# Order of the last retention head's rows and of the second feed-forward's first weights in a two-layer transformer kernel

## The chip, the cores and the metric

The kernel runs on one core of one Trainium2 chip. Its time is the device time of one execution in microseconds, taken over several runs; the median is given. All arithmetic is fp32 in effect: each large fp32 operand is split into a rounded high part (`hi`, made by ScalarE, type fp32r) and the remainder (`lo`, made by VectorE), and one product is three matmuls: hi x hi, lo x hi, hi x lo.

The engines are named as in the profile: PE (TensorE matmuls), PEld (its weight loads), DVE (VectorE), ACT (ScalarE), POOL (GpSimd) and SP (SyncE, which issues the transfers). SBUF is the on-chip memory, PSUM the eight banks into which PE writes.

## The reference

Two layers of a diffusion backbone over 512 latent tokens of width 1024 with 256 context tokens. Layer 0 is windowed attention with a feed-forward, for latent and context tokens; layer 1 is a bidirectional retention mixer with a feed-forward, for the latent tokens alone. The change lies at the end of the mixer of layer 1 and the start of its feed-forward:

```python
def gated_out(o, g):                      # per head: 512 columns
    mu = jnp.mean(o, axis=-1, keepdims=True)
    var = jnp.mean(jnp.square(o - mu), axis=-1, keepdims=True)
    y = ((o - mu) * lax.rsqrt(var + EPS)).reshape(...) * gn_gain
    return (jax.nn.silu(g) * y) @ w_o
...
x = x + mx[2] * out_x
h = modulate(rms_norm(x, norm2_g[i]), mx[3], mx[4])
gate, up = jnp.split(h @ w_in, 2, axis=-1)
x = x + mx[5] * ((jax.nn.silu(gate) * up) @ w_out)
```

The mixer has 4 heads, the feed-forward 2816 hidden columns, which are 22 tiles of 128.

## The kernel before

**Who sets the order.** The kernel is written as a straight program, and a planner (the tile scheduler) gives each engine its own queue: among the instructions that could start by its model it prefers those that stand first in the program. It adds the semaphore waits that the data and the buffers need. `after(ins, others)` adds an edge that orders the plan only: `ins` is not planned before `others`. On one engine this fixes the order in the queue; between two engines it puts no wait into the program. Each engine executes its queue strictly in order, so an instruction whose operand is late holds up all behind it.

**Weights.** All weights come as 128x1024 fp32 blocks in one stream (`w_raw`), mostly into two buffers `wraw`. ACT casts a block to its high part (`whi`), DVE subtracts for the low part (`wlo`), and only then is the raw buffer free for the next transfer on SP's queue. `next_w` (L136 to L142) does these three steps; `first_weights` (L1594) does them for the first weights of the feed-forward, `split` (L164 to L166) does the two computing steps for a block that is there.

**The last head (L1500 to L1585).** `ov` are four PSUM banks (X, X, Y, Y) with the retention output of four groups of 128 tokens, normalised in place (L1530). `gate` are the four gate tiles; the first two still need the product `Zg` added (L1562). `gated(n)` is a silu on ACT and a multiplication on DVE (L1536) that reads `ov[n]`, whose bank is then free. `transposes(i)` turns the gated tiles of tokens half i on PE (L1547) into banks `tps`: four banks X, X, Y, Y for e = 0 to 3, each with all 512 tokens. `turned(c)` splits the turned rows of half c, scaled by the norm's gain, into `yt[e]`: ACT the high part (L1552), DVE the low part (L1553). In the last head the half with tokens 256 to 511 is turned first and the other behind the fourth output tile.

**The output tiles (L1574 to L1630).** `out_tile(d, c)` makes 12 matmuls (L148, L149, L150 through `mm3`) for columns tile d and token half c, into banks pj and Z for the first half made (tokens 256 to 511) and X and Y for the other, and DVE adds the result to the residual stream (L1582). The weights of the eight tiles are four blocks, `w`. Among the tiles stand the squares for the second norm (L207 to L210), its scale (`rms`: a matmul with ones L217, then Ln, Exp and Square on ACT at L101 and L196, and two DVE steps L197 and L198) and the norms `second_norm` (L239 and L243 on DVE, L242 on ACT).

**The feed-forward (L1632 on).** `first_two` makes the hidden tiles f = 0 and 1, first for tokens 256 to 511 and then, behind `second_half` (scale and norms of the other tokens), for tokens 0 to 255. The hidden tile f = 2 is made by `plain`, all later ones by `seven`, a scheme of seven quarter products (L908) with sums of tokens (`token_sums`, L1228 to L1241, into `sA`) and of weights (`quarter_sums`, L915 to L918). `output` multiplies a group of hidden tiles with the output weights into the two pj banks and adds them to the residual stream on DVE (L253). In program order `output` of the first group stands between `plain` for f = 2 and `seven` for f = 3.

## Time and profile before

| | |
|---|---|
| median of 3 runs | 1764.6 us (1764.58 to 1765.39) |
| profiled execution | 1763.84 us |
| its span, first to last instruction | 1762.1 us |
| mean granted TensorE clock | 0.995 |
| PE busy | 1716.5 us (97%) |
| DVE busy | 1335.7 us (76%) |
| ACT busy | 844.1 us (48%) |
| POOL busy | 121.0 us (7%) |

Times in the profile are microseconds from the span's start. A timeline row has the start, the duration, engine, line, operation, written tile <- read tiles, shape, count, and in brackets the idle time of the engine before it with the engine, tile and line that ended it. A row with x2 or x3 merges so many instructions. A row of waits has the waiting engine, tile and line, what it waited for, the total, the number and the longest. Matmuls are pipelined: they start every 0.12 us (256 columns) or 0.23 us (512 columns), and a row's duration of 0.28 or 0.39 us overlaps the next.

### The profile page before, as it was taken

Reading aid. Unit: us, or ns where it says so; the run is one execution under the profiler, and the core shown is the slowest. Engines: PE = TensorE matmul, PEld = TensorE weight load, DVE = VectorE, ACT = ScalarE, POOL = GpSimd, SP = SyncE. Lnnn points to the kernel's source line nnn. Section 1 sums busy time; section 2 is a strip of 40 time slices with the busy share of each in tenths; the row PEclk is TensorE's granted clock in tenths of the full one; section 3 lists DMA queues with packets and bytes.
Section 4 is the critical chain, followed back from the end, with each engine's and each line's share of the span. In section 5 each row is a group of like instructions: output and inputs, shape, how many; then the busy total and the mean of one; then the engine's idle time right before and its main releaser. Section 6 shows DMA issues by size and latency. Waiting matters only on the chain. (4 is left out here: it accounts for less than half of the span.)

```text
span 1762.1 us, 28136 instructions
## 1 busy us (share of the span) xinstructions
PE 1716.5 (97%) x11082; PEld 1535.7 (87%) x11082; DVE 1335.7 (76%) x2373; ACT 844.1 (48%) x1504; POOL 121.0 (7%) x267
## 2 busy tenths in 40 slices
PE   6999999999999999999998999999999999999999
PEld 4788787889999999999987888897897889999998
DVE  6687786478778787877899758758768897777774
ACT  5467786364434333343565534524525564445442
POOL 0014344000000000000000000000000000000000
PEclk9999999999999999999999999999999999999999
DMA  9510014143343434343433434434433323233322
GB/s 354 224 49 14 18 59 153 49 132 108 96 132 124 140 121 155 108 144 128 124 110 122 155 104 128 153 109 132 145 107 109 96 85 115 89 108 108 98 83 84
DMA packets 60900, 205.67 MB, mean 117 GB/s; under 512 B 6752, under 2 KB 7136, under 8 KB 60640
## 3 DMA queue, kind: packets, MB, share of 16 engines
q1 hardware_dynamic: 53856, 178.71, 30.8%
q0 software_dynamic: 6912, 25.17, 4.6%
q8 instruction: 87, 1.43, 0.3%
q14 instruction: 45, 0.37, 0.1%
HBM read 201.75 MB, written 2.10 MB: 116 GB/s over the span
## 5 line engine op out<-in xcount | busy, mean ns | idle before, releaser
L165 ACT CAST whi<-wraw 128x1024 fp32r<-128x1024 f32 x173 | 181.4, 1051 | 309.0 <-PE Z L150 71.0
L166 DVE TENSOR_TENSOR wlo<-wraw,whi 128x1024 fp32r<-128x1024 f32 x173 | 211.1, 1222 | 36.1 <-ACT whi L165 35.5
L908 PE MATMUL Y<-aq,whi 128*128 128x384 f32 x640 | 173.9, 336 | 1.2 <-ACT hn L1049 1.2
L253 DVE SCALAR_TENSOR_TENSOR res<-pj,mod,res 128x512 f32<-128x512 f32 (+1 forms) x102 | 74.3, 730 | 77.7 <-PE pj L150 76.8
L141 DVE TENSOR_TENSOR wlo<-wraw,whi 128x1024 fp32r<-128x1024 f32 x77 | 94.1, 1222 | 34.6 <-ACT whi L140 32.9
L908 PEld LDWEIGHTS Y<-aq,whi 128*128 128x128 f32 x640 | 116.6, 188 | 3.0 <-ACT hn L1049 2.3
L140 ACT CAST whi<-wraw 128x1024 fp32r<-128x1024 f32 x77 | 80.9, 1050 | 74.5 <-PE Z L150 22.5
L271 DVE CUSTOM_DVE_ANT_0 y<-adaw,crow,small_sb 128x1024 bf16<-128x1024 f32 x64 | 81.9, 1280 | 34.4 <-DMA adaw<-in_adaT_dram 34.2
L908 PE MATMUL Y<-aq,wlo 128*128 128x384 f32 x320 | 107.1, 335 | 0.0
L1293 PE MATMUL Z<-whi,sA 128*128 128x512 f32 x256 | 80.7, 391 | 0.0
L101 ACT ACTIVATE pr<-pr,stat,qs 128x513 f32<-128x513 f32 (+2 forms) x96 | 74.2, 775 | 12.3 <-DVE stat L691 9.7
L698 POOL TENSOR_SCALAR pr<-pr,stat 128x512 f32<-128x512 f32 (+2 forms) x96 | 65.5, 696 | 76.4 <-DVE stat L695 57.5
L148 PE MATMUL pj<-ax,whi 128*128 128x512 f32 x176 | 68.8, 391 | 1.7 <-DVE res L253 1.7
L150 PE MATMUL pj<-ax,whi 128*128 128x512 f32 x176 | 68.6, 390 | 0.0
L149 PE MATMUL pj<-ax,wlo 128*128 128x512 f32 x176 | 68.5, 389 | 0.0
L268 POOL DMA_DIRECT2D adaw<-in_adaT_dram x48 | 25.6, 533 | 515.4 <-DVE mod L271 420.8
L148 PE MATMUL pj<-act,whi 128*128 128x512 f32 (+1 forms) x156 | 60.0, 385 | 0.4 <-DVE res L1122 0.4
L908 PE MATMUL Y<-sA,whi 128*128 128x256 f32 x304 | 60.3, 282 | 0.0
L908 PEld LDWEIGHTS Y<-aq,wlo 128*128 128x128 f32 x320 | 60.1, 188 | 0.1
L149 PE MATMUL pj<-act,wlo 128*128 128x512 f32 (+1 forms) x156 | 59.9, 384 | 0.0
L150 PE MATMUL pj<-act,whi 128*128 128x512 f32 (+1 forms) x156 | 59.5, 382 | 0.0
L685 DVE CUSTOM_DVE_ANT_0 pr<-S,mask,qs 128x256 f32<-128x256 f32 (+1 forms) x96 | 52.5, 567 | 8.3 <-PE S L684 5.1
(561 smaller groups left out, 5307.7 us busy)
## 6 DMA issues: line engine op xcount, KB each, us to landing
wraw<-in_wst_dram SPq DMA_DIRECT2D x234, 512.0 KB, 3.7
adaw<-in_adaT_dram POOLq DMA_DIRECT2D x48, 512.0 KB, 3.9
wx<-in_wst_dram SPq DMA_DIRECT2D x28, 512.0 KB, 3.9
adan<-in_adaQ_dram SPq DMA_DIRECT2D x16, 512.0 KB, 8.2
adan<-in_adaN_dram SPq DMA_DIRECT2D x16, 512.0 KB, 8.0
res<-in_xT_dram SPq DMA_DIRECT2D x16, 256.0 KB, 4.8
q<-in_adaN_dram SPq DMA_DIRECT2D x16, 256.0 KB, 3.3
aq<-in_adaN_dram SPq DMA_DIRECT2D x12, 256.0 KB, 6.2
```

The costliest lines, as they stand in the source:

```text
L101: ins = nc.scalar.activation(*args, **kw)
L140: nc.scalar.copy(hi, raw)
L141: nc.vector.tensor_tensor(lo, raw, hi, op=sub)
L148: after(nc.tensor.matmul(o, whi, xhi, start=first, stop=False), behind)
L149: nc.tensor.matmul(o, wlo, xhi, start=False, stop=False)
L150: return nc.tensor.matmul(o, whi, xlo, start=False, stop=last)
L165: nc.scalar.copy(hi, t)
L166: return nc.vector.tensor_tensor(lo, t, hi, op=sub)
L253: return nc.vector.scalar_tensor_tensor(res[d], o, mods[l, s][:, part, d:d + 1], res[d], mult, add)
L271: after(nc.vector.tensor_tensor_reduce(junk, w, cr[:, s * 1024:(s + 1) * 1024], 1.0, sm_t[:, C_ADAB + l * 48 + j:C_ADAB + l * 48 + j + 1], ...
L908: ins = nc.tensor.matmul(o, p, r, start=first and k + i == 0, stop=k == 3 and i == 2, skip_group_check=not first)
L1293: ins = nc.tensor.matmul(o, p, r, start=first and k + i == 0, stop=k == 3 and i == 2, skip_group_check=not first)
```

## The change

- `transposes` in the last head: tokens half 1 is turned into the two Y banks and half 0 into the two X banks, two rows e to a bank, 256 columns each, instead of four banks with 512 columns each for both.
- `turned` returns the last high and low part. In the last head the addition to gate[1] is ordered behind the last low part of half 1, the third output weight's cast behind its last high part, the fourth's behind the gating of gate[1].
- The low parts of the second pair of feed-forward weights are ordered behind the norms 6 and 7 of tokens half 1.
- The casts of the weights for f = 2 are ordered behind the Square in the scale of half 0, the token sums behind norm 7.
- In `seven` for f = 3 the low part of `u` is ordered behind the first residual addition of the first output, that of `g` behind the second.

No instruction is added or removed.

```diff
--- before.py
+++ after.py
@@ -133,11 +133,11 @@
         wsel[0] += 1
         return T(pool, 1024, "whi", bufs, F32R), T(pool, 1024, "wlo", bufs, F32R)
 
-    def next_w(pool, own=2, raw=None):
+    def next_w(pool, own=2, raw=None, behind=()):
 
         raw = raw or w_raw()
         hi, lo = w_parts(pool, own)
-        nc.scalar.copy(hi, raw)
+        after(nc.scalar.copy(hi, raw), behind)
         nc.vector.tensor_tensor(lo, raw, hi, op=sub)
         return hi, lo
 
@@ -193,9 +193,10 @@
 
         lnexp(y, tot, AF.Ln, scale=1.0 / count, bias=eps)
         lnexp(y, y, AF.Exp, scale=-0.5)
-        nc.scalar.activation(z, y, AF.Square, scale=0.5 / math.sqrt(count))
+        square = nc.scalar.activation(z, y, AF.Square, scale=0.5 / math.sqrt(count))
         nc.vector.scalar_tensor_tensor(z, tot, count * EPS, z, add, mult)
         nc.vector.scalar_tensor_tensor(y, z, -0.75, y, add, mult)
+        return square
 
     ssq = [None, None]
 
@@ -215,7 +216,7 @@
         n = y.shape[1]
         tot = bank()[:, :n]
         after(nc.tensor.matmul(tot, ones, y, start=True, stop=True), behind)
-        neg_half_rstd(y, t_sq(n), tot, D)
+        return neg_half_rstd(y, t_sq(n), tot, D)
 
     hpool = [None]
 
@@ -1533,34 +1534,40 @@
 
         def gated(n):
             silu(gate[n], gate[n])
-            nc.vector.tensor_tensor(gate[n], ov[n], gate[n], op=mult)
+            return nc.vector.tensor_tensor(gate[n], ov[n], gate[n], op=mult)
 
 
         tps = []
         yt = [(t_qk(), t_qk()) for _ in range(4)]
 
         def transposes(i):
-            if not tps:
+            if last:
+                a, b = W4("XY"[i]), W4("XY"[i])
+                tps[:] = [t[:, c] for t in (a, b) for c in HALVES]
+            elif not tps:
                 tps.extend((W4("X"), W4("X"), W4("Y"), W4("Y")))
             for n in (2 * i, 2 * i + 1):
+                c0 = (n - 2 * i if last else n) * P
                 for e in range(4):
-                    nc.tensor.transpose(tps[e][:, n * P:(n + 1) * P], gate[n][:, e * P:(e + 1) * P], ident)
+                    nc.tensor.transpose(tps[e][:, c0:c0 + P], gate[n][:, e * P:(e + 1) * P], ident)
 
         def turned(c):
             for e, (hi, lo) in enumerate(yt):
                 gn = sm_t[:, C_GN + hd * 4 + e:C_GN + hd * 4 + e + 1]
-                nc.scalar.activation(hi[:, c], tps[e][:, c], AF.Identity, scale=gn)
-                nc.vector.scalar_tensor_tensor(lo[:, c], tps[e][:, c], gn, hi[:, c], mult, sub)
+                t = tps[e] if last else tps[e][:, c]
+                high = nc.scalar.activation(hi[:, c], t, AF.Identity, scale=gn)
+                low = nc.vector.scalar_tensor_tensor(lo[:, c], t, gn, hi[:, c], mult, sub)
+            return high, low
 
         gated(2)
         gated(3)
         if last:
             transposes(1)
-            turned(HALVES[1])
+            rows = turned(HALVES[1])
         product_v(Zg, quarter_of(4), w22, False, (1,))
         for t in range(2):
-            nc.vector.tensor_tensor(gate[t], gate[t], Zg[t], op=add)
-            gated(t)
+            after(nc.vector.tensor_tensor(gate[t], gate[t], Zg[t], op=add), rows[1:1 + t] if last else ())
+            last_gate = gated(t)
         if not last:
 
             b11, Yv, vt, ins = values_first(first_weights_v(hd + 1))
@@ -1585,18 +1592,18 @@
             for d in range(KT):
                 out_tile(d, slice(0, SX))
             continue
-        w += [next_w(qp) for _ in range(4)]
+        w += [next_w(qp, behind=((), (), rows[:1], [last_gate])[i]) for i in range(4)]
         H.close()
         hM, hW, hX = (ctx.enter_context(tc.tile_pool(name=n, bufs=1, reuse_waits="tile", side="right"))
                       for n in ("hM", "hW", "hX"))
         ahead = []
 
-        def first_weights(room, behind=()):
+        def first_weights(room, behind=(), low=()):
             raw = w_raw()
             hi, lo = room()
             ahead.append((hi, lo))
             after(nc.scalar.copy(hi, raw), behind)
-            nc.vector.tensor_tensor(lo, raw, hi, op=sub)
+            after(nc.vector.tensor_tensor(lo, raw, hi, op=sub), low)
 
         wx_parts = lambda: (T(qw, 1024, "wx", 4, F32R), T(qw, 1024, "wx", 4, F32R))
         hW_parts = lambda: (T(hW, 1024, "whi", 2, F32R), T(hW, 1024, "wlo", 2, F32R))
@@ -1626,11 +1633,13 @@
                 if i == 1 and d > 3:
                     after(ins, done[d - 4:d - 3])
         done += [second_norm(k, HALVES[1]) for k in (KT - 2, KT - 1)]
-        for _ in range(2):
-            first_weights(hW_parts, done[5:6])
+        for i in (6, 7):
+            first_weights(hW_parts, done[5:6], done[i:i + 1])
+
+    scaled = []
 
     def second_half(behind):
-        rms(0, HALVES[0], behind=behind)
+        scaled.append(rms(0, HALVES[0], behind=behind))
         for k in range(KT):
             second_norm(k, HALVES[0])
 
@@ -1677,7 +1686,7 @@
             project(w[1], half(i), uo[:, c])
         return finish(go, uo)
 
-    def seven():
+    def seven(added):
         g, u = w_raw(fp, 2), w_raw()
         b11 = w_parts(fp, 4)
         b22 = T(hM, 512, "hm", 8, F32R), T(hM, 512, "hm", 8, F32R)
@@ -1685,8 +1694,8 @@
         split(g, *b11)
         split(u[:, 512:1024], *b22)
         quarter_sums(g, u)
-        split(u, *b32)
-        split(g, *b14)
+        after(split(u, *b32), added[0:1])
+        after(split(g, *b14), added[1:2])
         X, Y, Z = (T(psF, 512, n, 2)[:, 0:SC] for n in "XYZ")
         t, up = t_hn(SX), t_sq(SX)
         e1, e2 = T(rp, 512, "res", 12), T(rp, 512, "res", 12)
@@ -1724,23 +1733,23 @@
             for k in range(gsz):
                 c0 = k * nd * P + (d % nd) * P
                 mm3(o, (wd[0][:, c0:c0 + P], wd[1][:, c0:c0 + P]), acts[k], k == 0, k == gsz - 1)
-            gated_add(0, 1, 5, d, o, xr)
+            added.append(gated_add(0, 1, 5, d, o, xr))
             if final:
                 nc.sync.dma_start(out[:, d, :], xr[d])
 
     first = first_two()
-    f, prev = 0, None
+    f, prev, added = 0, None, []
     for gsz in FFN_GROUPS:
         acts = []
         for i in range(gsz):
             if f < 2:
                 acts.append(first[f])
             elif f == 2:
-                w = [next_w(fp), next_w(fp)]
-                token_sums(hm, 3, sh2, sA)
+                w = [next_w(fp, behind=scaled), next_w(fp, behind=scaled)]
+                token_sums(hm, 3, sh2, sA, done[7:8])
                 acts.append(plain(w))
             else:
-                acts.append(seven())
+                acts.append(seven(added if f == 3 else []))
             if i == 0 and prev is not None:
                 output(prev, False)
             f += 1
```

## The prediction

> **What bounds the kernel now.** I read the page first, then the busy time by stretches of 10 us around the code that the change touches, then the waits of TensorE there, and last the timelines of PE, DVE and ACT at each wait.
>
> ```profile
> span 1762.1 us, 28136 instructions
> ...
> PE 1716.5 (97%) x11082; PEld 1535.7 (87%) x11082; DVE 1335.7 (76%) x2373; ACT 844.1 (48%) x1504; POOL 121.0 (7%) x267
> ```
>
> PE is busy for 97% of the span, so a change of order can win only time in which PE stands still or runs slowly. The whole change lies between 1376 us (gating of the last retention head) and 1462 us (first output of the second feed-forward). The stretches (columns: length, PE, PEld, DVE, ACT, POOL, PEclk, DMA share, GB/s):
>
> ```profile
> 1380.00:1390.00 10.00, 7.83 (x45) 6.58 (x44) 7.51 (x12) 6.89 (x10) 0.00 (x0) 0.83 0.60 186
> 1390.00:1400.00 10.00, 10.00 (x86) 10.00 (x86) 8.37 (x21) 5.02 (x12) 0.00 (x0) 1.00 0.61 206
> 1400.00:1410.00 10.00, 10.00 (x84) 9.95 (x84) 7.82 (x19) 5.45 (x14) 3.87 (x8) 1.00 0.04 16
> 1410.00:1420.00 10.00, 8.93 (x72) 8.46 (x71) 8.50 (x17) 5.98 (x11) 2.02 (x3) 1.00 0.33 95
> 1420.00:1430.00 10.00, 9.01 (x71) 8.27 (x69) 9.59 (x21) 7.14 (x13) 0.00 (x0) 1.00 0.36 118
> 1430.00:1440.00 10.00, 10.00 (x89) 10.00 (x90) 10.00 (x22) 7.81 (x13) 0.00 (x0) 1.00 0.01 2
> 1440.00:1450.00 10.00, 10.00 (x80) 9.55 (x79) 9.72 (x13) 4.49 (x7) 0.00 (x0) 1.00 0.33 105
> 1450.00:1460.00 10.00, 8.27 (x42) 6.93 (x41) 9.97 (x15) 3.16 (x5) 0.00 (x0) 1.00 0.37 107
> ```
>
> PE has four holes (2.17, 1.07, 0.99 and 1.73 us), and in the first of them the granted clock is also low. DVE has 2.49+1.63+2.18+1.50 = 7.8 us free before 1420 us and only 0.41+0.00+0.28+0.03 = 0.7 us after: it is the engine to watch. PE's waits between 1360 and 1500 us (total, times, longest) name the holes:
>
> ```profile
> PE pj L148 <- ACT qk L1552: 2.1, 2, 1.8
> PE pj L148 <- DVE res L253: 1.7, 1, 1.7
> PE X L150 <- DVE hx L243: 1.1, 2, 0.6
> PE X L148 <- ACT hx L242: 0.8, 1, 0.8
> ```
>
> That is 5.7 us, and each row is one part of the change.
>
> **Part 1, the last head's rows.** PE's timeline, the first and the last row of 26 instructions (6 transposes, 20 matmuls) and the next row; then two stretches; then ACT and DVE:
>
> ```profile
> 1381.10 0.44 PE L1547 MATMUL X<-const_sb,gate 128*128 128x128 f32 x2
> ...
> 1388.50 0.28 PE L150 MATMUL pj<-qk,whi 128*128 128x256 f32 x1
> 1388.62 0.28 PE L148 MATMUL pj<-qk,whi 128*128 128x256 f32 x1
> ```
> ```profile
> 1381.50:1384.90 3.40, 1.58 (x11) 1.33 (x11) 2.48 (x4) 3.05 (x4) 0.00 (x0) 1.00 0.48 151
> 1384.90:1388.30 3.40, 3.05 (x15) 2.65 (x14) 2.37 (x5) 2.96 (x6) 0.00 (x0) 0.50 0.54 159
> ```
> ```profile
> 1378.04 0.68 DVE L1536 TENSOR_TENSOR gate<-Y,gate 128x512 f32<-128x512 f32 x1
> ...
> 1380.37 0.68 DVE L1536 TENSOR_TENSOR gate<-X,gate 128x512 f32<-128x512 f32 x1
> ...
> 1384.05 0.48 DVE L1553 SCALAR_TENSOR_TENSOR qk<-X,small_sb,qk 128x256 fp32r<-128x256 f32 x1
> 1384.45 0.68 DVE L1536 TENSOR_TENSOR gate<-X,gate 128x512 f32<-128x512 f32 x1
> ```
> ```profile
> 1381.83 1.04 ACT L140 CAST whi<-wraw 128x1024 fp32r<-128x1024 f32 x1 [1.85 <-DMA wraw<-in_wst_dram]
> 1382.78 0.47 ACT L1552 ACTIVATE qk<-X,small_sb 128x256 fp32r<-128x256 f32 x1
> ...
> 1386.25 0.84 ACT L1552 ACTIVATE qk<-X,small_sb 128x256 fp32r<-128x256 f32 x2
> ```
>
> Now the tokens of the second half are turned into four banks, and the two X banks hold ov[0] and ov[1] until their gating is done. So row e=0 waits for the gating at 1380.37 and then behind a weight cast that itself waits for its transfer; row e=1 waits for the gating at 1384.45. From 1381.10 to 1388.50 us PE does work that at the pace of the last two rows (0.12 us) takes 26 x 0.12 = 3.1 us: 7.4 - 3.1 = 4.3 us are lost. Of this, 3.4 us at clock 0.50 are 1.7 us.
>
> After the change the eight transposes of this half go to the two Y banks, free when the gating of 1378.04 ends (1378.7). The four high parts go to ACT from 1381.83 - 1.85 = 1379.98 on, into the 1.85 us in which it stood waiting (four at half of 0.84 are 1.7 us). The third weight's cast then starts at 1382 to 1382.5 instead of 1381.83. The low parts (0.48 us) follow the gating of 1380.37. The new cost is that two rows now share a bank. How such a pair behaves is seen in the first head, where two halves of one bank are split by ACT and DVE in turn:
>
> ```profile
> 934.17 0.41 DVE L166 TENSOR_TENSOR rkc<-X,rkc 128x256 fp32r<-128x256 f32 x1
> ```
> ```profile
> 934.61 0.37 ACT L165 CAST rkc<-X 128x256 fp32r<-128x256 f32 x1 [1.67 <-DVE rkc L166]
> ```
>
> ACT's read of the second half starts 0.03 us after DVE's read of the first ends (934.58), having waited for it. So a bank costs 2 x (0.47+0.48) = 1.9 us in series; with the two banks staggered all is done in 2.4 us, without in 3.3 us, that is at 1382.4 to 1383.8 counted from 1380 and the 1380.37 gating. The product ends at about 1381.3; PE then has the first rows for three output tiles (9 x 0.12 = 1.1 us), so 0 to 1.0 us of wait remains. I take 0.3, nearer the staggered order, and a gain of 4.0 us (3.3 to 4.3). The add to gate[1] goes behind the last low part, at 1382.5 to 1384; with silu and gating (0.6 to 0.7 us each) it ends before 1386. What it feeds, the first half's rows, is wanted when the second half's 96 output matmuls (11.5 us) are done, near 1393. The fourth weight, held behind that gating, is wanted by the seventh of the eight tiles (six at 12 x 0.12 us, 8.6 us after the start, near 1390). So both are covered by about 4 us of PE work.
>
> The Trainium skill (PSUM — Partial Sum Buffer, section "PSUM bank collisions raise a hardware error") states that two engines must not be in one bank at once, reads included, whichever columns they touch. This speaks against two banks for four rows, and the two rkc rows agree: this program keeps its readers apart. By the rule the wait of 0 to 1.0 us above has to be reckoned with; without it the rows would be out at 1382 and part 1 would win its full 4.3.
>
> **Part 2, the first feed-forward weights.** DVE, then PE:
>
> ```profile
> 1414.13 1.21 DVE L1599 TENSOR_TENSOR wlo<-wraw,whi 128x1024 fp32r<-128x1024 f32 x1
> 1415.27 0.47 DVE L243 SCALAR_TENSOR_TENSOR hx<-hm,mod,hx 128x256 fp32r<-128x256 f32 x1
> ```
> ```profile
> 1415.79 0.39 PE L150 MATMUL X<-hx,wx 128*128 128x256 f32 x1 [0.52 <-DVE hx L243]
> ...
> 1417.32 0.38 PE L150 MATMUL X<-hx,wx 128*128 128x256 f32 x1 [0.56 <-DVE hx L243]
> ```
>
> A weight's low part of 1.21 us stands ahead of the sixth and again of the seventh norm, and PE waits for both. The change puts norm 6 and norm 7 each ahead of one low part. Norm 6 wins 1.2 us, norm 7 the same (one low part may still stand between them). Of 0.52+0.56 = 1.1 us I take 1.0 (0.8 to 1.1); a token sum that now runs among the norms also goes behind. The low parts come about half a microsecond (one norm, 0.47) later and are wanted after the first projection.
>
> **Part 3, the scale of the first half's norm.** ACT, then PE:
>
> ```profile
> 1415.08 0.47 ACT L101 ACTIVATE y<-pj,small_sb 128x256 f32<-128x256 f32 x1
> 1418.88 1.05 ACT L140 CAST whi<-wraw 128x1024 fp32r<-128x1024 f32 x1 [3.32 <-DMA wraw<-in_wst_dram]
> 1419.83 0.41 ACT L101 ACTIVATE y<-y 128x256 f32<-128x256 f32 x1
> ```
> ```profile
> 1424.56 0.39 PE L148 MATMUL X<-hx,wx 128*128 128x256 f32 x1 [0.85 <-ACT hx L242]
> ```
>
> Between logarithm and exponential ACT waits 3.32 us for a weight transfer and casts it. Held behind the square, this cast can't stand there: the scale comes some 4.3 us earlier, far more than the 0.85 us of wait. Gain 0.9. The held cast is paced by its transfer anyway.
>
> **Part 4, the residual adds.** DVE, then PE:
>
> ```profile
> 1449.12 1.22 DVE L166 TENSOR_TENSOR wlo<-wraw,whi 128x1024 fp32r<-128x1024 f32 x1
> ...
> 1452.60 1.40 DVE L253 SCALAR_TENSOR_TENSOR res<-pj,mod,res 128x512 f32<-128x512 f32 x2
> ```
> ```profile
> 1453.39 0.50 PE L148 MATMUL pj<-ax,whi 128*128 128x512 f32 x1 [1.73 <-DVE res L253]
> ...
> 1461.78 0.28 PE L908 MATMUL Z<-sA,whi 128*128 128x256 f32 x1
> ```
>
> Both pj banks are full while DVE makes low parts that are first used after the eight output tiles (1461.78). With the first add ahead of one and the second ahead of the other, the first add comes up to 3 us earlier and the 1.73 us go; the cover, some 9 us, stays. Gain 1.7.
>
> Sum: 4.0+1.0+0.9+1.7 = 7.6 us; by the bounds 3.3+0.8+0.9+1.7 = 6.7 to 4.3+1.1+0.9+1.7 = 8.0. The printed waits start at modelled ends (0.39 us a matmul, against a pace of 0.12), which may hide 0.27 us at each of the last four: 1.1 more, 9.1 at most. Behind 1462 us PE is the bound, so this reaches the end. The profiled execution took 1763.84 us with its span of 1762.1; it becomes 1756.2. The median shown, 1764.6, is 0.8 higher: forecast **1757.0 us**. About 0.2% (3.5 us) is what a measurement of this kernel can tell from no change, so "faster" ends at 1761.1.
>
> **Rivals.** *DVE becomes the bound.* Ahead of the fourth hole PE would come 5.9 us earlier and DVE, nearly full after 1420 us, must follow by using up its 7.8 free us. If the chains through the norm scales keep half of these, DVE moves 3.9 us and PE waits the other 2.0 at a norm or an output weight: 5.6 us remain, 1759.0. For it speaks the DVE column from 1420 on; against it, that most of DVE's idle time is waiting for PE and ACT, which come earlier. Chance 0.19.
>
> *The edges steer only partly.* They bind the planner's order and put no wait into the program; if it places the second half's rows behind casts or transposes late, hole 1 stays and 3.6 us are won (1761.0), less if another hole stays (1762). Against it: today's transposes stand within a fraction of a microsecond of their gating. Chance 0.10.
>
> *The clock falls anyway.* In the stretch before the fall PE was busy 1.58 of 3.40 us; if what closes the clock is not this hole, its 1.7 us stay and 5.9 us are won, 1758.7. For it: PE waited as long at 1453.39, and PEclk of that stretch is 1.00; against it: the first hole is followed by a second wait within the same stretch, which the change removes too. Chance 0.04. The Trainium skill (TensorE: Matmul & The Clock Gate, Part 1) has the clock halve after a window of about 3.4 us that is idle; PE was not idle for all of it here, so the trace is stricter than the page.
>
> *Slower: the low parts of the second pair of weights slip behind the first half's norms in DVE's queue.* The edges hold them back, and the scale is now early, so those norms (a pair is 2 x 0.47 us, eight are 7.5) may be queued first. With all eight ahead: the scale is ready four steps of some 0.43 us after 1419.83 - 4.3, at 1417.2, the norms end at 1424.7, two low parts at 1427.1, against 1416.9 today (1415.27, norm at pace 0.4, low part 1.21). PE stands 10.2 us and loses 1.7 to the clock: 11.9 - 7.6 = 4.3 slower, 1768.9. It turns the sign from four pairs on (11.9 - 4 x 0.94 = 8.1). Against it: today these low parts stand even ahead of norms that precede them in the program. Chance 0.06.
>
> **How the numbers follow.** The forecast has 0.61. Faster by over 0.2%: forecast, clock and DVE case and a tenth of the partly steered one: 0.85. Within: most of the partly steered case and the mild end of the slower one, 0.11. Slower: 0.04. The range runs from 9.1 us won (1755.5, and 0.3 for the spread of the runs), 1755.2, to the upper end of the partly steered case's gain, 1761.5; inside lie the forecast, the DVE and the clock case and some of the third, 0.86.
>
> **What would show it.** Right: no PE wait on L148 behind the turned rows and PEclk 1.00 in every stretch after 1380; Ln, Exp and Square of the first half back to back on ACT; norms 6 and 7 ahead of the last low part; two residual adds before the last two low parts of the next group's weights; DVE free for under 5 us before 1420. Wrong: PE waits of over 1 us on hx or on wlo between 1400 and 1450, or clock 0.50 anywhere there.

## The result, and the profile after

| | before | changed |
|---|---|---|
| median of 11 runs | 1764.0 us (1760.77 to 1765.39) | 1760.25 us (1755.5 to 1762.35) |
| ratio, 95% interval | | 0.9976 (0.9967 to 0.9984) |
| profiled execution, its span | 1763.84, 1762.1 us | 1758.98, 1757.2 us |

The changed kernel is 4.2 us faster (2.8 to 5.8, from the ratio). It was forecast to be so, but by 7.6 us: little more than half of the sum arrived, and the rest of this text asks where the other half went. The page and the stretches of the changed kernel (columns: length, PE, PEld, DVE, ACT, POOL, PEclk, DMA share, GB/s):

```profile
PE 1716.2 (98%) x11082; PEld 1537.7 (88%) x11082; DVE 1335.0 (76%) x2373; ACT 843.3 (48%) x1504; POOL 121.4 (7%) x267
```
```profile
1380.00:1390.00 10.00, 10.00 (x84) 9.87 (x84) 9.12 (x18) 8.87 (x16) 0.00 (x0) 1.00 0.52 157
...
1410.00:1420.00 10.00, 8.43 (x65) 7.75 (x64) 7.38 (x18) 4.90 (x10) 0.00 (x0) 0.98 0.34 107
1420.00:1430.00 10.00, 10.00 (x75) 10.00 (x75) 10.00 (x22) 5.08 (x8) 0.00 (x0) 0.85 0.32 105
...
1440.00:1450.00 10.00, 9.53 (x59) 8.37 (x58) 9.37 (x14) 4.90 (x7) 0.00 (x0) 1.00 0.10 26
```

The hole at 1380 and its low clock are gone. The hole at 1450 has shrunk to 0.47 us and now lies ahead of 1450. But 1410 to 1420 now has a hole of 1.57 us, and the clock is low behind it. PE's waits between 1360 and 1500 us name the two that are left:

```profile
PE X L148 <- ACT hx L243: 1.5, 1, 1.5
PE pj L148 <- DVE res L254: 0.5, 1, 0.5
```

The first is part 3's own wait (it was 0.8), now twice as long. ACT, then DVE, then PE at that place (the lines of the changed kernel lie one to nine below the old ones: L243 is the norm's high part, L240 and L244 its steps on DVE, L1606 the low parts of the first feed-forward weights, L254 the residual add):

```profile
1410.65 0.42 ACT L196 ACTIVATE sq<-y 128x256 f32<-128x256 f32 x1
1413.78 1.06 ACT L140 CAST whi<-wraw 128x1024 fp32r<-128x1024 f32 x1 [2.70 <-DMA wraw<-in_wst_dram]
1417.16 1.04 ACT L140 CAST whi<-wraw 128x1024 fp32r<-128x1024 f32 x1 [2.33 <-DMA wraw<-in_wst_dram]
1418.11 2.10 ACT L243 ACTIVATE hx<-hm,mod 128x256 fp32r<-128x256 f32 x5
```
```profile
1408.87 1.21 DVE L1606 TENSOR_TENSOR wlo<-wraw,whi 128x1024 fp32r<-128x1024 f32 x1
1410.01 0.48 DVE L244 SCALAR_TENSOR_TENSOR hx<-hm,mod,hx 128x256 fp32r<-128x256 f32 x1
1410.40 1.22 DVE L1606 TENSOR_TENSOR wlo<-wraw,whi 128x1024 fp32r<-128x1024 f32 x1
...
1414.03 2.07 DVE L240 SCALAR_TENSOR_TENSOR hm<-res,acol,y 128x256 f32<-128x256 f32 x5
1418.65 1.68 DVE L244 SCALAR_TENSOR_TENSOR hx<-hm,mod,hx 128x256 fp32r<-128x256 f32 x4 [2.55 <-ACT hx L243]
```
```profile
1418.67 0.38 PE L148 MATMUL X<-hx,wx 128*128 128x256 f32 x1 [1.55 <-ACT hx L243]
```

Logarithm, exponential and square are indeed back to back and the scale is done at 1414.0. But the two casts for f = 2 now stand behind the Square and ahead of all eight high parts, and each waits for its transfer (2.70 and 2.33 us). The first high part comes at 1418.11; DVE, which has its part of the norms ready at 1414.5, stands still for 2.55 us, and PE for 1.55. The transfers could not be issued sooner in this order: SP issues them at 1410.15 and 1411.69, each 0.07 us after a low part of the weights before has ended (1408.87 + 1.21 and 1410.40 + 1.22) and its raw buffer is free; the first of them:

```profile
1410.15 0.33 SPq L122 DMA_DIRECT2D wraw<-in_wst_dram  x1
```

**A measure for single profiles.** The program ahead of the change is the same everywhere and still takes up to 4.7 us more or less from one execution to the next (the mark below lies between 1366.45 and 1371.17 us). So I count from a mark, the last head's first batch-norm statistics, to the first matmul of the second feed-forward ("ff"), to the first output tile behind f = 2 ("out") and to the end of the span. For the changed kernel:

```profile
1366.86 1.38 DVE L1522 BATCH_NORM_STATS2 y<-X 128x6 f32<-128x512 f32 x2 [1.27 <-PE X L1489]
```
```profile
1404.82 0.28 PE L148 MATMUL X<-hx,wx 128*128 128x256 f32 x1
```
```profile
1443.21 0.40 PE L148 MATMUL pj<-ax,whi 128*128 128x512 f32 x1
```

That is 37.96, 76.35 and 1757.2 - 1366.86 = 390.34 us. For the kernel before the first two of these rows are the following, which gives 42.33 and 1762.1 - 1367.87 = 394.23 us:

```profile
1367.87 1.38 DVE L1521 BATCH_NORM_STATS2 y<-X 128x6 f32<-128x512 f32 x2 [1.27 <-PE X L1488]
```
```profile
1410.20 0.28 PE L148 MATMUL X<-hx,wx 128*128 128x256 f32 x1
```

The same for every kernel that ran:

| kernel | median, us | ratio to before | to ff | to out | to end |
|---|---|---|---|---|---|
| before | 1764.0 | 1 | 42.33 | 79.59 | 394.23 |
| changed | 1760.25 | 0.9976 (0.9967 to 0.9984) | 37.96 | 76.35 | 390.34 |
| changed, second profile | 1758.14, one run | | 37.96 | 74.61 | 389.95 |
| part 1 alone | 1760.72 | 0.9982 (0.9971 to 0.9993) | 37.96 | 76.09 | 390.43 |
| part 2 alone | 1763.45, one run | | 41.68 | 78.36 | 394.53 |
| part 3 alone | 1763.87, one run | | 41.85 | 77.76 | 395.02 |
| part 4 alone | 1763.15, one run | | 41.83 | 79.75 | 393.13 |
| changed without part 3 | 1759.5 | 0.9972 (0.9962 to 0.9981) | 37.96 | 74.62 | 389.8 |
| casts behind norm 7 | 1757.75 | 0.9963 (0.995 to 0.9975) | 37.96 | 72.72 | 387.55 |
| casts behind norm 3 | 1756.89 | 0.9962 (0.9949 to 0.9976) | 37.96 | 72.71 | 387.86 |
| adds first only | 1761.16, one run | | 37.95 | 74.14 | 388.23 |
| both: norm 7, adds first | 1757.07 | 0.9948 (0.9935 to 0.9962) | 37.95 | 72.71 | 386.3 |
| both: norm 3, adds first | 1756.8 | 0.995 (0.9938 to 0.9962) | 37.96 | 72.71 | 386.24 |
| banks alone in part 1 | 1757.86, one run | | 38.2 | 74.05 | 389.52 |

The four kernels without part 1 have the same code up to "ff" and differ there by 0.65 us, so a difference of one profile below 0.7 us is read as nothing. Two things in the one profile of before stand behind much of it, and they pull against each other. Its first hole closed the clock; in the profiles of parts 2, 3 and 4 alone the same hole left it at 1.00, and they reach "ff" 0.48 to 0.65 us earlier. And ahead of "out" its PE ran for 17 us at a slightly faster pace than in those three (the last section), which is worth 0.67 us. The times come from five groups of runs, each with its own runs of before; they are compared through the ratio alone.

### The profile page after: what moved, and what is told of

It is laid out like the page before. It is cut to its first block, busy times and chain, and to the rows that moved or that the text cites. A ratio compares the mean times of both kernels' runs of the same rounds, so it can differ in the third digit from the quotient of the medians.

```text
span 1757.2 us, 28137 instructions
## 1 busy us (share of the span) xinstructions
PE 1716.2 (98%) x11082; PEld 1537.7 (88%) x11082; DVE 1335.0 (76%) x2373; ACT 843.3 (48%) x1504; POOL 121.4 (7%) x267
## 5 line engine op out<-in xcount | busy, mean ns | idle before, releaser
L254 DVE SCALAR_TENSOR_TENSOR res<-pj,mod,res 128x512 f32<-128x512 f32 (+1 forms) x102 | 74.4, 730 | 77.6 <-PE pj L150 76.7
```

What stands on the lines that cost most here:

```text
L254: return nc.vector.scalar_tensor_tensor(res[d], o, mods[l, s][:, part, d:d + 1], res[d], mult, add)
```

## The experiments

**Are the casts on ACT what was lost?** Two versions differ from the changed kernel only in what the f = 2 casts are ordered behind: not the Square but a norm of tokens half 0, the last or the fourth.

```diff
         for k in range(KT):
-            second_norm(k, HALVES[0])
...
+        scaled[:] = [second_norm(k, HALVES[0]) for k in range(KT)][7:8]     # first version
+        scaled[:] = [second_norm(k, HALVES[0]) for k in range(KT)][3:4]     # second version
```

> The casts of the weights for f = 2 are ordered behind the last norm of half 0 instead of behind the Square; all else as in the changed kernel. Theory A (the two casts, waiting 2.70 and 2.33 us for their transfers, stand ahead of the first high parts of half 0 on ACT and make PE's new hole of 1.8 us, which then halves the clock for 3.4 us): the hole and the half clock vanish, 1.7 + 1.7 = 3.4 us less than the changed kernel, about 7.2 under the kernel before (1756.8 beside 1764.0); PEclk 1.00 from 1380 to 1460. Theory B (the norms of half 0 are late on DVE whatever ACT does): PE waits on hx from DVE instead, less than 1 us is won over the changed kernel. Theory C (the casts are now too late): PE waits on wlo at f = 2 or at the output weights, no gain.

> As the last one, but the casts stand behind norm 3 of half 0, in the plan behind six of its eight high parts. Theory A: as good as behind norm 7, 3.4 us under the changed kernel, if both transfers have landed by then (they landed at 1413.8 and 1417.2); should the second cast still wait, the last two high parts are late and up to 1 us of PE wait is left. Theory B: less than 1 us over the changed kernel.

In both the wait on the high parts is gone, "out" comes 3.6 us earlier than in the changed kernel and the end 2.8 and 2.5 us earlier. Against the second profile of the changed kernel, whose clock stayed whole, the end comes 2.4 and 2.1 us earlier, so the 3.4 us of theory A were too many. What is left are waits on the residual adds, 0.67 + 0.54 and 0.42 + 0.86 us. Casts behind six of the eight high parts do as well as casts behind all eight.

**Does part 3 as it is built win anything?** Its two edges (on the casts and on the token sums) are taken out.

```diff
-                w = [next_w(fp, behind=scaled), next_w(fp, behind=scaled)]
-                token_sums(hm, 3, sh2, sA, done[7:8])
+                w = [next_w(fp), next_w(fp)]
+                token_sums(hm, 3, sh2, sA)
```

> The changed kernel without its third part (neither casts nor token sums are held back). In the plan one cast then stands behind the Square, three high parts of half 0 follow, then the second cast and the other five. Theory A: the first cast waits for its transfer as before (about 2.7 us), but PE finds three k steps (2.1 us of work) when it arrives, so its hole shrinks from 1.8 us to under 1 and the clock stays whole: 1.5 to 3.4 us under the changed kernel. The prediction's view (part 3 is worth 0.9 us): 0.9 us slower than the changed kernel.

The end comes at 389.8 us, against 390.34 and 389.95 with part 3: it wins nothing. Neither the 1.5 to 3.4 us of theory A nor the loss of 0.9 us by the prediction's view came. ACT and PE of this version:

```profile
1414.49 0.42 ACT L196 ACTIVATE sq<-y 128x256 f32<-128x256 f32 x1
1418.53 1.05 ACT L140 CAST whi<-wraw 128x1024 fp32r<-128x1024 f32 x1 [3.63 <-DMA wraw<-in_wst_dram]
1419.49 1.31 ACT L243 ACTIVATE hx<-hm,mod 128x256 fp32r<-128x256 f32 x3
```
```profile
1415.16 0.39 PE L150 MATMUL X<-hx,wx 128*128 128x256 f32 x1 [0.56 <-DVE hx L244]
1427.07 0.38 PE L150 MATMUL X<-hx,wx 128*128 128x256 f32 x1 [0.73 <-DVE hx L244]
```

Two things are seen. Already without part 3 the planner puts the first cast behind the Square, once part 2 is there: the exponential is free without any edge. And one of the two waits that part 2 was to remove (0.56) is still there; in the changed kernel it goes only because part 3 orders the token sums, four more DVE steps among the norms, behind norm 7. Of part 3's two edges that one does the work: the changed kernel without the edge on the casts, which was not run, builds into the same program, instruction for instruction.

**Each part alone.** The other three parts are set back to before.

```diff
-            first_weights(hW_parts, done[5:6], done[i:i + 1])       # part 2
+            first_weights(hW_parts, done[5:6])
...
-                w = [next_w(fp, behind=scaled), next_w(fp, behind=scaled)]     # part 3
-                token_sums(hm, 3, sh2, sA, done[7:8])
+                w = [next_w(fp), next_w(fp)]
+                token_sums(hm, 3, sh2, sA)
...
-                acts.append(seven(added if f == 3 else []))         # part 4
+                acts.append(seven([]))
```

> The kernel before with the first part alone (rows turned into two banks, casts and the addition to gate[1] ordered). By the trace of the changed kernel, whose PE reaches the first feed-forward matmul 4.4 us earlier against the start of the last head, and by the prediction (4.0): 4.0 to 4.4 us under the kernel before, if the three later holes stay as they are (1.1, 0.9, 1.7). Rival (PE that comes early finds the later holes wider, since casts wait for transfers and DVE is full there): 1 to 2.5 us under the kernel before, with the holes at hx grown to over 2 us each.

> The kernel before with the second part alone (low parts of the second pair behind norms 6 and 7). Its plan has the first cast for f = 2 behind the Square and three high parts behind it, without any edge of part 3. Theory: the two waits at hx k = 6 and 7 (1.1 us) shrink to under 0.4 and the wait at the first high part of half 0 (0.85) goes too, since the exponential no longer stands behind a cast: 1.0 to 2.0 us less from norm statistics to end than before (394.2). Rival (only the two waits are touched): 0.7 to 1.1 less, the wait of 0.85 stays.

> The kernel before with the third part alone. Its plan has both casts for f = 2 directly behind the Square, ahead of all eight high parts, as in the changed kernel. Theory (the harm comes from the meeting with an early PE): the transfers land as before, near 1419 and 1421.3, the high parts begin at about 1422.3, and PE, which is not early here, wants them at about 1423.5: no hole, 0.8 to 1.4 us less from norm statistics to end than before. Rival (the order is bad by itself): a wait of 1 us or more at the first high part and no gain.

> The kernel before with the fourth part alone (low parts of u and g for f = 3 behind the first and second residual addition). Prediction: the wait of 1.73 us for L253 goes, 1.7 us less from norm statistics to end. Theory after the first runs (in the changed kernel 0.47 us were left, with weight sums and a low part still ahead of the additions): 0.4 to 1.0 us of wait stay, 0.9 to 1.5 us less.

Part 1 alone: 4.37 us earlier at "ff", 3.8 at the end (a little under the 4.0 to 4.4 expected), as good as the whole change. Part 2 alone and part 3 alone: 1.2 and 1.8 us earlier at "out", of which 0.65 and 0.48 lie ahead of "ff", where the code is the same, and nothing won at the end (394.53 and 395.02 against 394.23), where I had expected 1 to 2 and 0.8 to 1.4 us. Where the gains of parts 2 and 3 go is seen in PE's waits; part 2 alone, then part 3 alone:

```profile
PE pj L148 <- DVE res L254: 2.6, 1, 2.6
...
PE X L150 <- DVE hx L244: 1.3, 2, 0.7
```
```profile
PE pj L148 <- DVE res L254: 2.5, 1, 2.5
PE X L150 <- DVE hx L244: 0.6, 1, 0.6
```

The wait for the residual adds was 1.7 before and has grown by 0.9 and 0.8 us: PE comes earlier by more than the adds do. In part 3 alone this longer wait also closed the clock: it is 0.50 from 1450.73 to 1454.14 us, which the three other kernels without part 1 do not have there, so its end says little of the order. Part 2 alone removes only the wait behind the exponential; two waits on norms, 1.3 us, are there as before (1.1). Part 3 alone has both casts ahead of all high parts and yet no wait at the first high part: counted from "ff" its second cast starts 1.5 us earlier than in the changed kernel (1419.77 - 1408.93 = 10.84 against 12.34), and PE, with the one norm wait that is left, comes 0.7 us later. So the order of the casts costs PE time where PE is early and the transfer late.

Part 4 alone: no wait on the adds is left, where I had expected 0.4 to 1.0 us of it. From "out" to the first product behind the eight output tiles it takes 1460.72 - 1448.02 = 12.70 us instead of 1461.78 - 1447.46 = 14.32, so 1.6 us are won at the place itself; at the end 1.1 are seen, since PE ran faster in other stretches of the profile of before (the last section).

**Both ends mended.** Beside the casts behind norm 7 the third sum of `quarter_sums` is now held behind the first residual add, the low part of `u` behind the second and that of `g` behind the fourth.

```diff
-        quarter_sums(g, u)
-        after(split(u, *b32), added[0:1])
-        after(split(g, *b14), added[1:2])
+        after(quarter_sums(g, u), added[0:1])     # quarter_sums returns its third sum
+        after(split(u, *b32), added[1:2])
+        after(split(g, *b14), added[3:4])
```

> As e1 (casts behind norm 7 of half 0), and for f = 3 more is held behind the first residual additions: the third weight sum behind the first, the low part of u behind the second, that of g behind the fourth. Theory: what is left of the fourth hole in e1 (0.67 and 0.54 us of wait for L254, since weight sums and a low part still stood ahead of the additions) goes; 1.0 to 1.4 us under e1, that is about 8 us under the kernel before, and 386.2 to 386.6 us from the start of the last head's norm statistics to the end (before 394.2, changed 390.3, e1 387.6). Rival: DVE is full there, the held pieces come late and PE waits at the first products of f = 3 instead: as e1 or slower.

1757.07 us, ratio 0.9948: about 9 us faster than before (6.7 to 11.5) and 7.93 us by the mark. This beats both kernels. PE's only wait between 1360 and 1500 us is 0.2 us behind all that was changed; DVE is busy through the place where the changed kernel idles; the second add comes 1.9 us behind the first instead of 3.1 (waits of PE, a stretch, DVE):

```profile
PE Y L909 <- ACT res L1708: 0.2, 1, 0.2
```
```profile
1410.00:1420.00 10.00, 10.00 (x83) 9.67 (x82) 9.93 (x22) 5.39 (x12) 0.00 (x0) 1.00 0.36 107
```
```profile
1443.60 0.75 DVE L254 SCALAR_TENSOR_TENSOR res<-pj,mod,res 128x512 f32<-128x512 f32 x1
...
1445.50 0.75 DVE L254 SCALAR_TENSOR_TENSOR res<-pj,mod,res 128x512 f32<-128x512 f32 x1
1446.16 0.68 DVE L919 TENSOR_TENSOR wraw<-wraw 128x512 f32<-128x512 f32 x1
```

> The f=2 casts behind the fourth half-0 norm, and the residual adds first as in the version with the casts behind the last norm. Theory (it only matters that no cast stands ahead of the first high parts): as that version, 1757.1 us within 1 us, 386.3 to 386.6 us from the first batch-norm statistics to the end, no TensorE wait above 0.5 us between 1380 and 1460. Rival (a cast in the middle of the norms waits for its transfer and holds the last four): a wait of 0.5 to 1.5 us on a high part near 1422 to 1426.

With the casts behind the fourth norm it is the same (1756.8 us, 386.24): the rival's wait near 1422 to 1426 does not appear, and it is enough that the casts stand behind the first six high parts.

**The adds first, the casts left as they are.** The second of the two edits alone.

> The changed kernel with the weight sums of the last pair of weights held behind the first residual add and the two low parts behind the second and the fourth; the f=2 casts stay where the change leaves them, ahead of the eight half-0 high parts on ACT. My theory (the lost time is mainly the casts on ACT): the wait of 1.5 to 1.8 us on the high part and the half-clock stretch after it stay, the 0.47 us at the residual adds goes, and from the first batch-norm statistics to the end it takes 389.6 to 390.0 us against 390.3 of the changed kernel and 394.2 of the kernel before. Rival (the adds are what gave the gain back): as low as the version with both mended, 386.3.

388.23 us, outside what my theory gave (389.6 to 390.0) and short of the rival's 386.3. So the casts are not "mainly" the loss: with them left as they are, the adds give 2.1 us against the changed kernel's first profile; with the adds already mended, the casts give 388.23 - 386.3 = 1.9. Against the second profile of the changed kernel (389.95) the adds give 1.7. The two halves are about equal. Part of my error was the clock, which did not fall in this run: the same two casts stand ahead of the high parts, but the second came 0.6 us less late (2.64 and 1.73 us of waiting), and PE waited 0.88 us.

```profile
1418.02 1.05 ACT L140 CAST whi<-wraw 128x1024 fp32r<-128x1024 f32 x1 [2.64 <-DMA wraw<-in_wst_dram]
1420.80 1.05 ACT L140 CAST whi<-wraw 128x1024 fp32r<-128x1024 f32 x1 [1.73 <-DMA wraw<-in_wst_dram]
```

**Are the edges of part 1 needed?** The two shared banks stay; the orders of the gate's add and of the third and fourth weight go.

```diff
-            after(nc.vector.tensor_tensor(gate[t], gate[t], Zg[t], op=add), rows[1:1 + t] if last else ())
+            after(nc.vector.tensor_tensor(gate[t], gate[t], Zg[t], op=add), ())
...
-        w += [next_w(qp, behind=((), (), rows[:1], [last_gate])[i]) for i in range(4)]
+        w += [next_w(qp, behind=()) for i in range(4)]
```

> The changed kernel with the two shared banks for the turned rows, but without the order edges that put the low parts ahead of the add to the gate and the weights behind the rows. Theory (the order on ACT and DVE is needed as well): some row's high part stands behind a weight's cast that waits for its transfer, or behind silu; TensorE waits 1 to 2.5 us more there and the first feed-forward begins 39.5 to 42 us after the first batch-norm statistics instead of 37.96. Rival (the banks do it alone): 37.96, no wait at the rows.

The rival holds: 38.2 us to "ff" and no wait at the rows, though a cast stands between the second and third high part and the fourth comes 2.3 us later than the third. The edges are worth at most 0.24 us, which one profile does not resolve; the banks do all of it.

**The changed kernel once more.** Is the half clock part of the price?

> The changed kernel once more, unaltered, for a second profile of the wait at the first half-0 high part. In two other profiles with the same two casts ahead of the high parts TensorE waited 0.88 and 0.66 us there and the clock stayed whole; in the changed kernel's profile it waited 1.55 us and the next 3.4 us ran at half clock. Theory (the depth of the wait is set by when the second transfer lands, which moves from execution to execution, and the clock falls only for the deep ones): a wait of 0.6 to 1.6 us; with a wait under 1 us no half-clock stretch and the first output tile 74.0 to 74.3 us after the first batch-norm statistics and 388.2 to 389 us to the end, with one over 1.3 us a half-clock stretch, 76 to 76.5 and 390 to 390.5. Rival (something particular to the changed kernel, such as its add order, makes the wait deep): 1.5 us, half clock and 76.3 again.

Neither answer is quite right. PE waited 1.34 us, over the 1.3 for which I had expected the fall, and the clock stayed whole; the last section shows why the depth alone does not decide it. The first half of the theory holds: the second transfer is issued 6.87 us behind "ff" in the two profiles of the changed kernel and with the adds first, the cast that waits for it starts at 12.34, 12.14 and 11.68, and PE waits 1.55, 1.34 and 0.88 us. Why the transfer takes a different time in each is not shown. "out" came 1.74 us earlier than in the first profile. And yet the end is only 0.39 us earlier, because PE now waits for the adds (waits of PE, then DVE):

```profile
PE pj L148 <- DVE res L254: 1.8, 2, 0.9
PE X L148 <- ACT hx L243: 1.3, 1, 1.3
```
```profile
1418.04 2.08 DVE L244 SCALAR_TENSOR_TENSOR hx<-hm,mod,hx 128x256 fp32r<-128x256 f32 x5 [2.35 <-ACT hx L243]
...
1444.10 0.74 DVE L254 SCALAR_TENSOR_TENSOR res<-pj,mod,res 128x512 f32<-128x512 f32 x1
```

In the first profile the same two steps of DVE are those of 1418.65, above, and of 1444.80:

```profile
1444.80 0.75 DVE L254 SCALAR_TENSOR_TENSOR res<-pj,mod,res 128x512 f32<-128x512 f32 x1
...
1446.73 1.22 DVE L166 TENSOR_TENSOR wlo<-wraw,whi 128x1024 fp32r<-128x1024 f32 x1
1447.86 1.40 DVE L254 SCALAR_TENSOR_TENSOR res<-pj,mod,res 128x512 f32<-128x512 f32 x2
```

From the first norm to the first add DVE needs 1444.80 - 1418.65 = 26.15 us with the half clock on PE and 1444.10 - 1418.04 = 26.06 us without. In these stretches it is busy for 26.08 and 26.06 us (third number; columns as above):

```profile
1418.65:1444.80 26.15, 26.11 (x199) 25.63 (x200) 26.08 (x47) 17.71 (x29) 0.00 (x0) 0.93 0.24 81
```
```profile
1418.04:1444.10 26.06, 25.89 (x204) 24.85 (x204) 26.06 (x47) 17.48 (x29) 0.00 (x0) 1.00 0.27 81
```

DVE sets the time from hole to hole. In the first profile PE, at half clock for 3.41 us, used up most of the time that it spends waiting for the adds in the second, so the slow stretch cost next to nothing. What costs is that DVE begins late, after 2.55 or 2.35 us of idling, and that the second add stands behind a low part.

## Why the prediction was right in sign and short in size

**Part 1 (forecast 4.0 us, "its full 4.3" without the wait at the banks): right.** 42.33 - 37.96 = 4.37 us at "ff", and 3.7 to 3.9 against the three profiles in which the first hole left the clock whole. So the size is right, but the share of it that the prediction gave to the clock, 1.7 us, is not: the half clock was worth 0.48 to 0.65 us there, since at full clock PE only waits longer for the rows (2.4 to 2.6 us instead of 2.1). The first output tile follows the product's last matmul without a gap, and the clock is whole:

```profile
1380.28 0.40 PE L1294 MATMUL Z<-whi,sA 128*128 128x512 f32 x1
1380.52 0.28 PE L148 MATMUL pj<-qk,whi 128*128 128x256 f32 x1
```
```profile
1379.90 0.84 ACT L1558 ACTIVATE qk<-Y,small_sb 128x256 fp32r<-128x256 f32 x2 [0.55 <-DVE qk L1559]
1381.32 0.47 ACT L1558 ACTIVATE qk<-Y,small_sb 128x256 fp32r<-128x256 f32 x1 [0.58 <-DVE qk L1559]
```

The last rows show the price that the prediction allowed for shared banks: ACT stands 0.55 and 0.58 us until DVE has left the bank, as the rule of the Trainium skill (PSUM — Partial Sum Buffer, section "PSUM bank collisions raise a hardware error") lets expect. It cost PE nothing, because the rows began in time and the first tiles could run on the rows that were out. That the clock would fall anyway at this place is refuted: it is 1.00 from 1380 to 1390 us in every profile with part 1.

**Part 2 (1.0 us): the waits went, but not by this part alone.** Norms 6 and 7 stand ahead of the last low part, as forecast (DVE rows of 1410.01 and 1410.40). Without part 3's order of the token sums one of the waits, 0.56 us, stays, and the prediction mentioned these sums without pricing them.

**Part 3 (0.9 us): the step that failed.** It said: "Held behind the square, this cast can't stand there", and "The held cast is paced by its transfer anyway". Both are true, and the conclusion, a gain of 0.9 us, was wrong: the wait that was to go (0.85) came back as one of 1.55 and 1.34 us. ACT runs its queue in order, so a cast that is taken from ahead of the exponential has to stand somewhere else, and there it holds what is behind it. The scale is ready 2.6 us earlier against "ff" (1414.00 - 1404.82 = 9.2 us; before, 1421.55 + 0.42 - 1410.20 = 11.8, by the step of y on DVE and the first matmul; the 4.3 us forecast were too many, since the low part and the four token sums now stand on DVE between the Square, which ends at 1411.07, and the scale's two steps, which begin at 1413.12), but the first high part only half a microsecond earlier: 1418.11 - 1404.82 = 13.3 instead of 1424.00 - 1410.20 = 13.8, its row of before being the following.

```profile
1424.00 1.31 ACT L242 ACTIVATE hx<-hm,mod 128x256 fp32r<-128x256 f32 x3 [1.69 <-DVE hm L239]
```

I had priced what the cast holds up where it stood and not what it would hold up where it went, though the transfer's lateness (3.32 us) was in the quoted row. PE, without the waits of part 2, wants the high part at 1417.1 and gets it 1.55 us late.

**Part 4 (1.7 us): right alone, half a step in the changed kernel.** The order is as forecast, one add ahead of each low part, and in the kernel before it wins 1.6 us at its place. But in the changed kernel PE reaches the adds earlier against DVE. It alternates between two banks and needs the second add almost as soon as the first; with the low part of `u` ordered between them (1446.73, 1.22 us) it comes 3.1 us after the first. And all four sums of weights (0.68 us each) stand ahead of the first add; in the mended version two of them stand behind it (the last is the row of 1446.16). Mending that gave 1.3 and 1.6 us (387.55 to 386.3, 387.86 to 386.24) where the casts were mended too, 1.7 to 2.1 where they were not.

**The sum.** 7.6 us were forecast as four terms that add. By the mark 3.89 and 4.28 us came; part 1 alone brings 3.8. The terms 2 to 4 did not add, because DVE stands between the holes: what is won in front of it is waited for at the adds. With the two orders mended 7.93 and 7.99 us come, the size of the sum and its upper bound (8.0); by the ratio it is about 9 (6.7 to 11.5). So the four holes together were priced about rightly, and it was the edges that did not close two of them. That the mark gives the sum so closely is partly luck, as the half clock and the faster pace in the one profile of before work against each other.

**The rivals.** "DVE becomes the bound" names what happened in effect: it was to leave 5.6 us, and DVE does set the time from 1418 to 1445. It was meant as DVE running out of free time, though, and the runs show that it runs out because it idles 2.5 us behind ACT: the prediction's own sign, "DVE free for under 5 us before 1420", failed (0.88 + 1.78 + 0 + 2.62 = 5.3), and in the version with both mended it is met with about 2.7. The sign for "wrong", a wait of over 1 us on `hx` between 1400 and 1450, appeared as well, and so did the other, clock 0.50 (from 1419.51 to 1422.92 us, in the first profile). "The edges steer only partly" is right for part 3, whose edge on the casts moves nothing in the changed kernel. The slower case did not happen: one low part stands behind norm 6, the other behind norm 7, and both ahead of the half-0 norms.

## What to carry to other kernels

When an instruction that waits for a transfer is moved down an in-order queue, price what stands behind its new place, not only what is freed at the old one; put it behind the last instruction that anybody is waiting for. Gains of several holes on one path add only if the engine between them can follow: look whether it idles there for someone else. A producer that works into two buffers needs both freed early, so order the second release like the first.

## What the runs showed of the hardware

**When the clock halves.** In each trace the half-clock stretches begin on one grid with a step of 3.413 us. In the changed kernel's first profile they begin at 47.35, 119.03, 938.23 and 1419.51 us, which is 21, 240 and 141 steps apart. Where the grid lies against the program differs from execution to execution, but within a trace the window ahead of each fall can be laid out. The changed kernel's first profile and then its second, whose grid follows from a fall at 932.37 us:

```profile
1416.10:1419.51 3.41, 1.84 (x13) 1.43 (x12) 0.86 (x4) 2.35 (x5) 0.00 (x0) 1.00 0.01 5
1419.51:1422.92 3.41, 3.41 (x18) 3.41 (x17) 3.41 (x10) 2.44 (x6) 0.00 (x0) 0.50 0.00 0
```
```profile
1413.65:1417.07 3.42, 3.07 (x27) 2.86 (x25) 2.04 (x5) 1.13 (x2) 0.00 (x0) 1.00 0.29 113
1417.07:1420.48 3.41, 2.40 (x18) 2.20 (x19) 2.44 (x7) 2.53 (x6) 0.00 (x0) 1.00 0.00 0
1420.48:1423.89 3.41, 3.41 (x32) 3.41 (x31) 3.41 (x8) 2.59 (x4) 0.00 (x0) 1.00 0.00 0
```

In the first, the hole (1417.12 to 1418.67) lies inside one window: PE is busy for 1.84 of 3.41 us, far from idle, and the next window runs at 0.50. In the second, the hole (1416.72 to 1418.06) is cut in two by the grid at 1417.07, the windows keep 3.07 and 2.40 us, and the clock stays whole. So one program does both, and besides the depth of a hole its place on the grid counts. The first hole of the kernel before is such a case too: 1.59 us in its window and then half clock, but 1.80 and 2.52 us in two windows and full clock with part 2 alone.

The same can be counted over all windows at full clock between 27 and 1745 us in the fourteen traces, with PE's busy time by modelled ends. Behind a window with at most 1.69 us of work the clock fell in 27 of 29 cases, behind one with 1.70 to 2.35 us in 14 of 80, and behind a fuller one never. What decides between 1.70 and 2.35 us stays open.

**Two paces at the same granted clock.** At a granted clock of 1.00 three matmuls of 256 columns start 0.34 us apart in some stretches and 0.353 us in others. Ahead of "out" the same matmuls take 17.00 us in the profile of before and 17.67 us with part 4 alone. What sets the pace is not seen in the traces.
